# Stick-breaking heads: the value products placed behind nine products of the next projection, the weight tiles split by bank 1, 0, 2

## The chip, the cores and the metric

The kernel runs on one core of one Trainium2 chip. The metric is the device time of one execution in microseconds (us), taken as the median of several runs. Beside the times there is one execution recorded by the hardware profiler; its rows are what the profile shows. The engines are named as the profile names them: PE is TensorE (matrix products), PEld its weight loads, which run beside the products, DVE is VectorE, ACT is ScalarE, POOL is GpSimd, and SP is the engine whose queue issues most of the DMAs.

## The reference, cut to what matters

The kernel computes one transformer block on 512 tokens of width 1024. A conditioning vector gives six shift, scale and gate vectors. The normed and modulated input goes through one wide projection `w_in`, which feeds 16 stick-breaking attention heads (head size 64), 4 retention heads and two branch gates. Both branches are projected, gated, added and projected again, and a gated feed-forward with its own norm and a last norm follow. The change lies in the stick-breaking heads:

```python
def stick_breaking_attention(q, k, v):
    ...
    for i in range(s_len // BLOCK):
        end = (i + 1) * BLOCK
        ...
        z = jnp.einsum('bhtd,bhsd->bhts', qb, kb).astype(jnp.float32) * scale
        ...
        mask = s_pos[None, :] < t_pos[:, None]
        log_1m_beta = jnp.where(mask, jax.nn.log_sigmoid(-z), 0.0)
        after = lax.cumsum(log_1m_beta, axis=3, reverse=True) - log_1m_beta
        log_a = jax.nn.log_sigmoid(z) + after
        a = jnp.where(mask, jnp.exp(log_a), 0.0)
        outs.append(jnp.einsum('bhts,bhsd->bhtd', a.astype(v.dtype), vb))
    return jnp.concatenate(outs, axis=2)
```

For each head there are scores `z`, weights `a` (a product of sigmoids, taken from the right), and the sum of the values under these weights. Nothing of this arithmetic is changed.

## The kernel before, in words

Everything is float32. A product with nearly full precision is made of three products of rounded halves: a tensor is split into a high half (ACT copies it with rounding) and a low half (DVE subtracts the high half from the original), by `split` (L204 to L212, rows L206 on ACT and L208 on DVE). `mm3` (L230) multiplies high by high, high by low and low by high. `gemm` (L235) runs over the eight 128-row slices k of a weight tile and calls `mm3` for each, so 24 products of 512 columns make one projection of 128 output rows. All products pass through `mm`, whose line L228 therefore stands on nearly all PE rows; the tile names tell them apart: `ps<-h,whi` and `ps<-h,wlo` are products of a projection, `z<-q,q` scores, `ps<-con,s` and `av<-con,s` (L647) transposes, `av<-s,v` the value products.

The stick-breaking stage runs in the profile from about 480 to 670 us. `heads(h)` (L1125) is called for h = 0 to 16. One call does, for the head before it (n = h - 1), the transposes and splits (`sb_turn`, L640), then for head h the scores and sigmoids (`sb_front`, L617) and the scan (`sb_scan`, L634), and then the value products of head n (`sb_out`, L656). Between two calls stands projection work: `mix(1)` or `mix(2)` (one or two gate projections of 24 products, by `gate`, L810) or `sb_qk` (two projections, 48 products, the queries and keys of a later pair of heads). It has no connection with the head around it and gives PE something to do while DVE and ACT work on the head.

In a head, ten transposes bring the weights, a triangle of 128x128 blocks, into three PSUM tiles, called banks in the code: bank 0 (512 columns, `ps`), bank 1 (512 columns, `ps`) and bank 2 (256 columns, `av`). The blocks for key block j lie in bank 0 (j = 0), bank 1 (j = 1 and, from column 384, j = 3) and bank 2 (j = 2). Each bank is split into halves in SBUF (tag `s`), in the order 0, 1, 2 before. Eight value products follow: for each j two, one per half, of 512 - 128 j columns. They accumulate into one PSUM tile `o`, taken by `psa()`. The pool behind `psa()` has one buffer (`av=1`), and bank 2 of the transposes is taken by `psa()` too: `o` and bank 2 are the same PSUM memory, one after the other.

ACT then copies `o` out (L667), SP exchanges 64 rows (L669), and the next call of `heads` adds them up on DVE (`sb_sums`, L677).

A scheduler sets the order of the instructions on each engine when the program is built. It follows the order in which the code is written as far as its estimates of readiness allow, and fills gaps with work written later. Before, `sb_out` is written ahead of the projection; the scheduler draws 5, 6, 9 or 12 products of the projection ahead of the value products (5 for heads 0 and 1; 9 for 2, 4, 6, 8 and 10; 6 for 3, 5, 7, 9 and 11 to 14; 12 for 15).

Of the kernel before, what the change touches and what calls it, by code (L numbers as in the profile page):

```python
# [19 lines left out]
P = 128  # L20
D = 1024
S = 512
# [93 lines left out]
def kernel(  # L116
# [19 lines left out]
    def nm(s):  # L136
        uid[0] += 1
        return f"{s}_{uid[0]}"

    def ps():  # L140
        return pspool.tile([P, S], F32, tag="ps", bufs=BUFS["ps"], name=nm("ps"))

    def psa():
        return pspool.tile([P, S], F32, tag="av", bufs=BUFS["av"], name=nm("av"))
# [4 lines left out]
    def pair(tag):  # L149
        return apool.tile([P, 2, S], F32R, tag=tag, bufs=BUFS[tag], name=nm(tag))  # L150

    def tmp():
        return apool.tile([P, S], F32, tag="t", bufs=BUFS["t"], name=nm("t"))

    def otile():
        return apool.tile([P, S], F32, tag="o", bufs=BUFS["o"], name=nm("o"))
# [47 lines left out]
    def split(dst_hi, dst_lo, src, scale=1.0, eng=None):  # L204

        nc.scalar.activation(dst_hi, src, AF.Copy, scale=scale)  # L206
        if isinstance(scale, float) and scale == 1.0:
            return (eng or nc.vector).tensor_sub(dst_lo, src, f(dst_hi))  # L208
        return nc.vector.scalar_tensor_tensor(
            dst_lo, src, scale, f(dst_hi), op0=ALU.mult, op1=ALU.subtract  # L210
        )

    last_low = [None]

    def weight(key, eng=None):
        idx = WIDX[key]
        _, _, _, nk, cols = PLAN[idx]
        nc_cols = sum(n for _, n in cols)
        n = nk * nc_cols
        raw = load_raw(wp[idx], n)  # L220
        hi = wpool.tile([P, WCOLS], F32R, tag="whi", bufs=BUFS["whi"], name=nm("whi"))
        lo = wpool.tile([P, WCOLS], F32R, tag="wlo", bufs=BUFS["wlo"], name=nm("wlo"))
        last_low[0] = split(hi[:, :n], lo[:, :n], raw[:, :n], eng=eng)
        v = lambda t: t[:, :n].rearrange("p (k c) -> p k c", k=nk)
        return v(hi), v(lo)

    def mm(o, lhs, rhs, start, stop):
        return nc.tensor.matmul(o, lhs, rhs, start=start, stop=stop, skip_group_check=True).ins  # L228

    def mm3(o, lh, ll, rh, rl, start, stop):  # L230
        mm(o, lh, rh, start, False)
        mm(o, lh, rl, False, False)
        mm(o, ll, rh, False, stop)

    def gemm(o, w, acts, start=True, stop=True, t0=0, t1=S, ks=None):  # L235

        hi, lo = w
        n = len(acts)
        for k in ks or range(n):
            a = acts[k]  # L240
            ah, al = a if isinstance(a, tuple) else (a[:, 0, :], a[:, 1, :])
            mm3(o, hi[:, k, :], lo[:, k, :], ah[:, t0:t1], al[:, t0:t1],
                start and k == 0, stop and k == n - 1)


    def ada_raw(n, tag):
# [197 lines left out]
    with tc.manual_schedule(engines={nc.vector.engine, nc.scalar.engine, nc.tensor.engine}):  # L444
# [11 lines left out]
        c = sm[:, SM_C : SM_C + KT]  # L456
# [133 lines left out]
    def sb_qk(p):  # L590
        qp, kp = ps(), ps()
        gemm(qp, weight(("sq", p)), hs)
        gemm(kp, weight(("sk", p)), hs)
        low = last_low[0]
        sb_qk_store(p, qp, kp)
        return low
# [20 lines left out]
    def sb_front(h):  # L617
        q, k = sbq[h], sbk[h]
        z = [psz(), psz(), psz()]
        for i, bank, c, _ in reversed(SEG):  # L620
            w = (i + 1) * P
            for n in range(2):
                head_pe[h] = mm(z[bank][:, c : c + w], q[:, n, i * P : (i + 1) * P], k[:, 0:w],
                                n == 0 and c == 0, n == 1)
        n4, n1, b4, b1 = stick_sets[h % 2]
        for segs in ((3,), (2, 0), (1,)):
            for (t4, t1), scale in (((n4, n1), -1.0), ((b4, b1), 1.0)):
                for i, bank, c, at in (SEG[i] for i in segs):
                    w = (i + 1) * P - 1
                    t = t1 if i == 1 else t4  # L630
                    nc.scalar.activation(t[:, at : at + w], z[bank][:, c : c + w], AF.Sigmoid, scale=scale)  # L631
        return n4, n1, b4, b1

    def sb_scan(n4, n1, b4, b1):  # L634
        for n, b, d in ((n4, b4, diag), (n1, b1, diag[:, 640:896])):
            w = n.shape[-1]
            nc.vector.tensor_tensor_scan(n[:, ::-1], n[:, ::-1], d[:, ::-1], 0.0, op0=ALU.mult, op1=ALU.max)  # L637
            nc.vector.tensor_mul(b[:, 0 : w - 1], b[:, 0 : w - 1], n[:, 1:w])

    def sb_turn(n4, n1, b4, b1):  # L640
        at = [ps(), ps(), psa()]
        for i, _, _, a in reversed(SEG):
            t = b1 if i == 1 else b4
            for j in range(i + 1):
                bank, c = TGEO[j]
                c += (i - j) * P
                nc.tensor.transpose(at[bank][:, c : c + P], t[:, a + j * P : a + (j + 1) * P], ident)  # L647
        avs = []
        for bank in range(3):
            w = TBANKW[bank]  # L650
            hl = pair("s")
            ins = split(hl[:, 0, :w], hl[:, 1, :w], at[bank][:, :w])
            avs.append(hl)
        return avs, ins

    def sb_out(h, avs):  # L656
        vt = sbv[h // 4]
        o = psa()
        r, hf = (h % 4) // 2, h % 2
        for j in (3, 2, 1, 0):  # L660
            bank, c = TGEO[j]
            w = S - j * P
            v = vt[j // 2][:, j % 2, r * 256 + hf * P : r * 256 + hf * P + P]
            for i in range(2):
                mm(o[:, j * P : S], v, avs[bank][:, i, c : c + w], j == 3 and i == 0, j == 0 and i == 1)
        u, u2 = tmp(), tmp()
        nc.scalar.activation(u, o, AF.Copy)  # L667
        own, oth = (slice(0, HD), slice(HD, P)) if hf == 0 else (slice(HD, P), slice(0, HD))
        nc.sync.dma_start(u2[own], u[oth])  # L669
        late_sums.append((o_sb[h // 2], own, u, u2))  # L670
# [3 lines left out]
    def sb_sums():  # L674
        while late_sums:
            dst, own, u, u2 = late_sums.pop()
            nc.vector.tensor_add(dst[own], u[own], u2[own])  # L677
# [148 lines left out]
    def ret_mixed():  # L826
        while late_mixes:
            d, g, r = late_mixes.pop()
            nc.vector.tensor_mul(g, g, r)
            nc.sync.dma_start(spill[d], g)  # L830
# [272 lines left out]
    def sb_v(g):  # L1103

        sbv[g] = [pair("v") for _ in PI]
        for n, vt in enumerate(sbv[g]):
            nc.sync.dma_start(f(vt), vspill[2 * (g - 2) + n])
# [17 lines left out]
    def heads(h):  # L1125
        with tc.issue_after(act_table.ins):
            ins = act_table
            if h:
                if h % 8 == 1 and h > 8:
                    sb_v(2)  # L1130
                    sb_v(3)
                avs, ins = sb_turn(*fronts.pop(h - 1))
            if h < 16:
                fronts[h] = sb_front(h)
                sb_scan(*fronts[h])
            with tc.issue_after(ins.ins):
                sb_sums()
                ret_mixed()
            if h:
                if h % 2:  # L1140
                    o_sb[h // 2] = otile()
                sb_out(h - 1, avs)

    for h in range(17):
        heads(h)
        p = h // 2 + 2
        if p > 7:
            mix((1, 2, 2, 1, 2)[h - 12])
            if h == 16:
                sb_sums()  # L1150
        elif h % 2:
            mix(1)
        else:
            low_ = sb_qk(p)
            if h in (2,):
                ada_after(low_)
    ln_exp_tables()
    acts = []
    for j in range(8):
        hl = pair("q" if j < 4 else "s")  # L1160
# [3 lines left out]
    for d in range(8):  # L1164
        o = ps()
# [6 lines left out]
        hl = pair("h")  # L1172
# [326 lines left out]
    for d in range(4):  # L1499
        o = ps()  # L1500
# [191 lines left out]
    for d in FULL:  # L1692
        o = ps()
# [160 lines left out]
```

## Time and profile before

| | us |
|---|---|
| time, median of 3 runs | 1117.16 (1116.42 to 1117.90) |
| the profiled execution's own time | 1117.19 |
| its span, first to last instruction | 1115.3 |
| PE busy | 1102.8 |
| DVE busy | 871.5 |
| ACT busy | 560.7 |
| SP's DMA queue (q1), share of 16 DMA engines | 45.7% |

1.89 us of the profiled execution's own time lie outside its span. A busy PE in the table is no proof of a full PE: the end of a product is modelled and lies after the start of the next one, so that a short gap between starts does not show as idle time. Gaps are read from the starts of successive rows, and from the idle time ahead of a weight load. A timeline row has the start, the length, the engine, the line, the operation, the tiles written and read, and how many equal instructions were merged; idle time of the engine ahead of it stands in brackets.

### The profile page before, as it was taken

Reading aid. Unit: us, or ns where it says so; the run is one execution under the profiler, and the core shown is the slowest. Engines: PE = TensorE matmul, PEld = TensorE weight load, DVE = VectorE, ACT = ScalarE, POOL = GpSimd, SP = SyncE. Lnnn points to the kernel's source line nnn. Section 1 sums busy time; section 2 is a strip of 40 time slices with the busy share of each in tenths; the row PEclk is TensorE's granted clock in tenths of the full one; section 3 lists DMA queues with packets and bytes.
Section 4 is the critical chain, followed back from the end, with each engine's and each line's share of the span. In section 5 each row is a group of like instructions: output and inputs, shape, how many; then the busy total and the mean of one; then the engine's idle time right before and its main releaser. Section 6 shows DMA issues by size and latency. Waiting matters only on the chain.

```text
span 1115.3 us, 15035 instructions
## 1 busy us (share of the span) xinstructions
PE 1102.8 (99%) x5609; PEld 936.7 (84%) x5609; DVE 871.5 (78%) x1298; ACT 560.7 (50%) x925; POOL 40.6 (4%) x69
## 2 busy tenths in 40 slices
PE   9999999999999999999999999999999999999996
PEld 7888888888888888888888888889988888888886
DVE  7898966847867768488677775667999988988866
ACT  5455345445444645355565653357745544554443
POOL 0000000010020020000000000000000000000000
PEclk9999999999999999999999999999999999999999
DMA  9725751582485295888676449662444544434112
GB/s 364 297 78 185 241 188 66 169 207 77 155 179 176 78 208 187 215 237 236 177 201 166 137 152 309 240 177 58 127 138 117 149 132 132 133 113 132 58 38 76
DMA packets 59976, 181.41 MB, mean 163 GB/s; under 512 B 7424, under 2 KB 9472, under 8 KB 59904
## 3 DMA queue, kind: packets, MB, share of 16 engines
q1 hardware_dynamic: 53888, 166.30, 45.7%
q0 software_dynamic: 5472, 13.63, 7.8%
q8 instruction: 44, 0.72, 0.3%
q10 hardware_dynamic: 544, 0.52, 0.1%
q14 instruction: 28, 0.23, 0.1%
HBM read 148.97 MB, written 16.78 MB: 149 GB/s over the span
## 4 chain that ended last, share of the span: by engine, by line
PE 94%; DVE 3%; ACT 1%; DMA 0%; issue 0%; SPq 0%; DVEq 0%; ACTq 0%
PE ps L228 70%; PE z L228 14%; PE av L228 8%; PE ps L647 1%; DMA x<-xT 0%; PE z L782 0%; ACT q L1231 0%; PE av L647 0%; DVE o L1726 0%; DVE h L1541 0%; DVE t L778 0%; DVE s L1276 0%; DVE h L1276 0%; ACT h L1542 0%; DVE fin L1740 0%
## 5 line engine op out<-in xcount | busy, mean ns | idle before, releaser
L228 PE MATMUL ps<-h,whi 128*128 128x512 f32 (+1 forms) x1026 | 293.2, 372 | 0.0
L228 PEld LDWEIGHTS ps<-h,whi 128*128 128x128 f32 x1026 | 185.2, 189 | 32.2 <-issue 0.5
L206 ACT ACTIVATE whi<-raw 128x1024 fp32r<-128x1024 f32 (+1 forms) x104 | 108.7, 1046 | 196.0 <-PE ps L228 144.2
L228 PE MATMUL ps<-h,wlo 128*128 128x512 f32 (+1 forms) x513 | 187.9, 370 | 0.0
L208 DVE TENSOR_TENSOR wlo<-raw,whi 128x1024 fp32r<-128x1024 f32 (+1 forms) x104 | 124.9, 1201 | 66.8 <-ACT whi L206 66.5
L228 PEld LDWEIGHTS ps<-h,wlo 128*128 128x128 f32 x513 | 96.7, 188 | 16.6
L228 PE MATMUL ps<-s,whi 128*128 128x512 f32 x320 | 98.9, 390 | 0.0
L228 PE MATMUL ps<-q,whi 128*128 128x512 f32 (+1 forms) x368 | 98.5, 385 | 0.0
L878 DVE TENSOR_TENSOR wlo<-s,whi 128x1024 fp32r<-128x1024 f32 x46 | 56.2, 1223 | 43.2 <-ACT whi L874 43.2
L228 PEld LDWEIGHTS ps<-q,whi 128*128 128x128 f32 x368 | 68.0, 188 | 13.3
L874 ACT ACTIVATE whi<-s 128x1024 fp32r<-128x1024 f32 x47 | 49.8, 1059 | 50.2 <-PE ps L228 40.2
L228 PE MATMUL ps<-whi,h 128*128 128x512 f32 x222 | 71.8, 391 | 0.0
L228 PEld LDWEIGHTS ps<-s,whi 128*128 128x128 f32 x320 | 60.1, 188 | 12.7 <-DVE s L208 0.3
L228 PE MATMUL ps<-s,wlo 128*128 128x512 f32 x160 | 62.2, 389 | 0.0
L228 PE MATMUL ps<-q,wlo 128*128 128x256 f32 (+1 forms) x328 | 59.3, 293 | 0.0
L228 PEld LDWEIGHTS ps<-q,wlo 128*128 128x128 f32 x328 | 48.2, 190 | 3.3
L228 PEld LDWEIGHTS ps<-whi,h 128*128 128x128 f32 x222 | 41.7, 188 | 9.6 <-ACT t L1023 1.1
L228 PE MATMUL ps<-wlo,h 128*128 128x512 f32 x111 | 43.2, 389 | 0.0
L228 PE MATMUL ps<-whi,q 128*128 128x512 f32 x128 | 40.7, 389 | 0.0
L637 DVE TENSOR_TENSOR_SCAN s<-s,table 128x1024 f32<-128x1024 f32 x16 | 36.6, 2288 | 4.6 <-ACT s L631 4.5
L228 PE MATMUL z<-q,q 128*128 128x256 f32 (+3 forms) x224 | 40.1, 325 | 0.0
L228 PEld LDWEIGHTS z<-q,q 128*128 128x128 f32 x224 | 34.8, 189 | 3.0 <-DVE q L208 0.2
(353 smaller groups left out, 2187.5 us busy)
## 6 DMA issues: line engine op xcount, KB each, us to landing
raw<-wp SPq DMA_DIRECT2D x136, 512.0 KB, 3.8
araw<-wp SPq DMA_DIRECT2D x30, 512.0 KB, 4.2
s<-wp SPq DMA_DIRECT2D x24, 512.0 KB, 6.0
araw<-wada SPq DMA_DIRECT2D x18, 512.0 KB, 4.5
sraw<-wada SPq DMA_DIRECT2D x16, 512.0 KB, 9.0
q<-qp SPq DMA_DIRECT2D x32, 256.0 KB, 3.7
s<-wada SPq DMA_DIRECT2D x14, 512.0 KB, 7.2
spill<-o POOLq DMA_DIRECT2D x24, 256.0 KB, 4.4
```

What stands on the lines that cost most here:

```text
L206: nc.scalar.activation(dst_hi, src, AF.Copy, scale=scale)
L208: return (eng or nc.vector).tensor_sub(dst_lo, src, f(dst_hi))
L228: return nc.tensor.matmul(o, lhs, rhs, start=start, stop=stop, skip_group_check=True).ins
L637: nc.vector.tensor_tensor_scan(n[:, ::-1], n[:, ::-1], d[:, ::-1], 0.0, op0=ALU.mult, op1=ALU.max)
L647: nc.tensor.transpose(at[bank][:, c : c + P], t[:, a + j * P : a + (j + 1) * P], ident)
L874: nc.scalar.activation(hi, t, AF.Copy)
L878: last_low[0] = nc.vector.tensor_sub(lo, t, f(hi))
```

## The change

Two things are changed. First, `heads` no longer calls `sb_out` itself. It puts the call into a list, `due`, and `gemm` takes it from there and makes it after its third slice, that is behind nine products of the projection that comes next. Second, `sb_turn` splits the banks in the order 1, 0, 2, and `sb_out` makes the value products in the order j = 3, 1, 0, 2, so that both that read bank 1 come first, then the one of bank 0 and then the one of bank 2.

```diff
     last_low = [None]
+    due = []
...
             mm3(o, hi[:, k, :], lo[:, k, :], ah[:, t0:t1], al[:, t0:t1],
                 start and k == 0, stop and k == n - 1)
+            if k == 2 and due:
+                due.pop()()
...
-        avs = []
-        for bank in range(3):
+        avs = {}
+        for bank in (1,0,2):
             w = TBANKW[bank]
-            hl = pair("s")
+            avs[bank] = hl = pair("s")
             ins = split(hl[:, 0, :w], hl[:, 1, :w], at[bank][:, :w])
-            avs.append(hl)
         return avs, ins
...
-        for j in (3, 2, 1, 0):
+        for j in (3, 1, 0, 2):
             bank, c = TGEO[j]
             w = S - j * P
             v = vt[j // 2][:, j % 2, r * 256 + hf * P : r * 256 + hf * P + P]
             for i in range(2):
-                mm(o[:, j * P : S], v, avs[bank][:, i, c : c + w], j == 3 and i == 0, j == 0 and i == 1)
+                mm(o[:, j * P : S], v, avs[bank][:, i, c : c + w], j == 3 and i == 0, j == 2 and i == 1)
...
-                sb_out(h - 1, avs)
+                due.append(lambda: sb_out(h - 1, avs))
```

What the built programs have in a row is shown at three places. The first is PE after the scores of head 4, where the value products of head 3 come; `ps` is the projection, `h_205`, `h_245` and `h_291` are its first three slices, `s_4467`, `s_4470` and `s_4473` are the three split pairs of the head in the order in which they were made, and `v` the values. Before:

```order
L228 MATMUL ps_4515<-h_205,whi_4519 128x512 x2
L228 MATMUL ps_4515<-h_205,wlo_4520 128x512
L228 MATMUL ps_4515<-h_245,whi_4519 128x512 x2
L228 MATMUL ps_4515<-h_245,wlo_4520 128x512
L228 MATMUL av_4502<-s_4470,v_3645 128x128 x2
L228 MATMUL av_4502<-s_4473,v_3645 128x256 x2
L228 MATMUL av_4502<-s_4470,v_3511 128x384 x2
L228 MATMUL av_4502<-s_4467,v_3511 128x512 x2
L228 MATMUL ps_4515<-h_291,whi_4519 128x512 x2
L228 MATMUL ps_4515<-h_291,wlo_4520 128x512
```

The same place in the changed program:

```order
L229 MATMUL ps_4502<-h_205,whi_4506 128x512 x2
L229 MATMUL ps_4502<-h_205,wlo_4507 128x512
L229 MATMUL ps_4502<-h_245,whi_4506 128x512 x2
L229 MATMUL ps_4502<-h_245,wlo_4507 128x512
L229 MATMUL ps_4502<-h_291,whi_4506 128x512 x2
L229 MATMUL ps_4502<-h_291,wlo_4507 128x512
L229 MATMUL av_4519<-s_4467,v_3645 128x128 x2
L229 MATMUL av_4519<-s_4467,v_3511 128x384 x2
L229 MATMUL av_4519<-s_4470,v_3511 128x512 x2
L229 MATMUL av_4519<-s_4473,v_3645 128x256 x2
```

Three products of the projection have moved from behind the value products to ahead of them, and the 256-column pair, which reads the last split pair, has moved to the end. So it is for heads 3, 5, 7, 9 and 11 to 14; for heads 0 and 1 four products have moved.

The second place is PE at the value products of head 4, where nine products of the projection (`ps_4654` before, `ps_4641` now) stood ahead already. Before:

```order
L228 MATMUL ps_4654<-h_291,whi_4657 128x512 x2
L228 MATMUL ps_4654<-h_291,wlo_4658 128x512
L228 MATMUL av_4641<-s_4610,v_3650 128x128 x2
L228 MATMUL av_4641<-s_4613,v_3650 128x256 x2
L228 MATMUL av_4641<-s_4610,v_3516 128x384 x2
L228 MATMUL av_4641<-s_4607,v_3516 128x512 x2
```

The changed program at the same place:

```order
L229 MATMUL ps_4641<-h_291,whi_4644 128x512 x2
L229 MATMUL ps_4641<-h_291,wlo_4645 128x512
L229 MATMUL av_4657<-s_4607,v_3650 128x128 x2
L229 MATMUL av_4657<-s_4607,v_3516 128x384 x2
L229 MATMUL av_4657<-s_4610,v_3516 128x512 x2
L229 MATMUL av_4657<-s_4613,v_3650 128x256 x2
```

Only the order among the value products differs here; so it is for heads 2, 4, 6, 8 and 10, and for head 15 with its 12 products ahead.

The third place is DVE at the last three low halves of head 4, where `ps_4594` is bank 0, `ps_4595` bank 1 and `av_4596` bank 2. Before:

```order
L208 TENSOR_TENSOR s_4607<-ps_4594,s_4607 128x512
L208 TENSOR_TENSOR s_4610<-ps_4595,s_4610 128x512
L208 TENSOR_TENSOR s_4613<-av_4596,s_4613 128x256
```

In the changed program:

```order
L208 TENSOR_TENSOR s_4607<-ps_4595,s_4607 128x512
L208 TENSOR_TENSOR s_4610<-ps_4594,s_4610 128x512
L208 TENSOR_TENSOR s_4613<-av_4596,s_4613 128x256
```

Banks 0 and 1 have changed places; bank 2 is last as before. Apart from this, DVE, ACT and POOL have the same operations in the same order. In SP's queue one write of a gated tile (L830) now stands ahead of a load of values (L1107) instead of behind it, at two places. As for the semaphores: ahead of the first value product stood an instruction of PE that only waits (for DVE), and the product itself waited for an earlier count of PE; now the product waits for DVE itself, for the same subtraction of bank 2, and the 16 extra instructions are gone. ACT has 25 more instructions that only wait, most of them ahead of the splits, for counts of the head before.

## The prediction

> **What bounds the kernel now.** I read the page's first part, then the stretches of the heads and behind them, then PE's own waits, and last single rows.
>
> ```profile
> PE 1102.8 (99%) x5609; PEld 936.7 (84%) x5609; DVE 871.5 (78%) x1298; ACT 560.7 (50%) x925; POOL 40.6 (4%) x69
> 480.00:670.00 190.00, 189.60 (x975) 158.36 (x974) 145.97 (x178) 109.96 (x239) 0.00 (x0) 1.00 0.64 184
> PEld av L228 <- issue: 6.4, 16, 0.6
> ```
>
> PE is busy for 99% of the span and, in the stretch of the heads (columns: PE, PEld, DVE, ACT, POOL, granted clock, DMA share, GB/s), for 189.60 of 190 us at the full clock, with DVE at 146 us and ACT at 110. So PE's own sequence sets the time, and only what stretches that sequence can be won. In this stretch one wait of the weight loads is listed: the first load of the value products, 16 times, once a head, 6.4 us together. The view calls it "issue", that is, it names no releaser. The rows do. Head 3:
>
> ```profile
> 519.50 1.28 DVE L208 TENSOR_TENSOR s<-ps,s 128x512 fp32r<-128x512 f32 x2
> 520.61 0.19 PEld L228 LDWEIGHTS ps<-h,wlo 128*128 128x128 f32 x1
> 520.70 0.41 DVE L208 TENSOR_TENSOR s<-av,s 128x256 fp32r<-128x256 f32 x1
> 520.84 0.40 PE L228 MATMUL ps<-h,wlo 128*128 128x512 f32 x1
> 521.23 1.11 PEld L228 LDWEIGHTS av<-s,v 128*128 128x128 f32 x8 [0.43 <-issue]
> 522.61 0.61 PE L228 MATMUL ps<-h,whi 128*128 128x512 f32 x2
> ```
>
> The load at 521.23 follows the end of DVE's subtraction of bank 2 (520.70 + 0.41 = 521.11) by 0.12 us. The first product does not read bank 2: it reads bank 1, whose halves were done at 519.50 + 1.28 = 520.78. What it waits for is the memory of bank 2, which its output `o` takes over. Head 4, with nine products ahead already:
>
> ```profile
> 536.14 0.41 DVE L208 TENSOR_TENSOR s<-av,s 128x256 fp32r<-128x256 f32 x1
> 536.37 0.40 PE L228 MATMUL ps<-h,wlo 128*128 128x512 f32 x1
> 536.67 1.11 PEld L228 LDWEIGHTS av<-s,v 128*128 128x128 f32 x8 [0.33 <-issue]
> 538.04 0.40 PE L228 MATMUL ps<-h,whi 128*128 128x512 f32 x1
> ```
>
> The same 0.12 us: 536.55 to 536.67. Here the splits come later, because a projection's splits stand ahead of them on DVE.
>
> **What a wait costs.** A load runs ahead of its product, under the product before it, so part of the 0.43 us costs nothing. What counts is the time from the start of the last product ahead to that of the first one behind: 522.61 - 520.84 = 1.77 us for head 3, 538.04 - 536.37 = 1.67 for head 4. Without a wait the retention scores show it:
>
> ```profile
> 161.34 0.39 PE L228 MATMUL ps<-whi,qp 128*128 128x512 f32 x1
> 161.56 3.98 PE L228 MATMUL z<-q,q 128*128 128x128 f32 x24
> 165.38 0.39 PE L228 MATMUL ps<-whi,h 128*128 128x512 f32 x1
> ```
>
> These are six products each of 128, 256, 384 and 512 columns, in this order, behind a product of 512; the value products are two of each, in the same order. A third of 165.38 - 161.56 is 1.27, with the 0.22 ahead 1.50 us (estimated, rounded up). So head 3 loses 0.27 us and head 4 0.17: the listed wait less 0.16.
>
> ```profile
> 487.45 1.11 PEld L228 LDWEIGHTS av<-s,v 128*128 128x128 f32 x8 [0.38 <-issue]
> 496.83 0.76 PEld L228 LDWEIGHTS av<-s,v 128*128 128x128 f32 x6 [0.38 <-issue]
> 657.34 1.11 PEld L228 LDWEIGHTS av<-s,v 128*128 128x128 f32 x8 [0.43 <-issue]
> 618.18 1.10 PEld L228 LDWEIGHTS av<-s,v 128*128 128x128 f32 x8 [0.64 <-issue]
> 512.49 1.11 PEld L228 LDWEIGHTS av<-s,v 128*128 128x128 f32 x8 [0.33 <-issue]
> 666.77 1.11 PEld L228 LDWEIGHTS av<-s,v 128*128 128x128 f32 x8 [0.33 <-issue]
> ```
>
> Heads 0 and 1 wait 0.38 us, seven heads 0.43 (head 3 the first, 14 the last), head 11 0.64, and six 0.33 (2 the first, 15 the last).
>
> **The change, part by part.**
>
> *First term, products moved ahead.* Ten heads (0, 1, 3, 5, 7, 9, 11 to 14) get three or four more products of 0.23 us ahead, at least 0.68 us. In head 3 the load would then come at 520.84 + 0.68 = 521.52, 0.3 us after the 521.23 at which it may start today; in head 11 it would come at some 618.2, just at its 618.18. The waits vanish: 2 x 0.22 + 7 x 0.27 + 0.48 = 2.81 us. The six other heads have the same number ahead as before and keep their wait, 6 x 0.17 = 1.02 us, of which the new split order takes nothing: bank 2 is last as before. What is late next: ACT's copy of `o` and SP's exchange come 0.2 to 0.7 us later against PE. Behind that copy ACT has the next weight split:
>
> ```profile
> ACT whi L206 <- PE ps L228: 68.2, 21, 3.9
> v<-vspill SPq DMA_DIRECT2D x4, 512.0 KB, 4.5
> ```
>
> It waits for PE anyway, 68.2 us in 21 waits. If that cover were gone, some 0.5 us would be paid once per head. The swap in SP's queue, twice, delays a load of values that are used five heads later, some 60 us on; cost nothing. Used at once, they would hold PE for the 4.5 us of their landing (second row).
>
> *Second term, one instruction less.* The wait for DVE stood in an instruction of its own; now the load carries it. The row of a load that waits itself:
>
> ```profile
> 99.52 0.74 DVE L778 SCALAR_TENSOR_TENSOR t<-av,sm,t 128x512 f32<-128x512 f32 x1
> 100.32 0.31 PEld L782 LDWEIGHTS z<-con,t 128*128 128x128 f32 x3 [0.35 <-DVE t L778]
> ```
>
> 100.26 to 100.32, 0.06 us instead of 0.12. In the six heads that still wait this is worth 6 x 0.06 = 0.36 us; bounds 0 and 0.36.
>
> *Third term, the order among the value products.* Each row names the first of the products merged in it; the starts count.
>
> ```profile
> 521.51 0.63 PE L228 MATMUL av<-s,v 128*128 128x256 f32 x3
> 521.68 0.63 PE L228 MATMUL av<-s,v 128*128 128x256 f32 x3
> 521.80 0.74 PE L228 MATMUL av<-s,v 128*128 128x384 f32 x3
> 521.97 0.80 PE L228 MATMUL av<-s,v 128*128 128x384 f32 x3
> 519.63 0.68 PE L228 MATMUL ps<-h,whi 128*128 128x512 f32 x2
> 520.15 0.40 PE L228 MATMUL ps<-h,wlo 128*128 128x512 f32 x1
> 520.38 0.62 PE L228 MATMUL ps<-h,whi 128*128 128x512 f32 x2
> ```
>
> The first 256-column product behind the short ones takes 0.17 us, the second 0.12, and one of 384 0.17: loads have fallen behind in the 128-column pair, and the next product pays 0.05 us unless it is 0.17 long itself. Now a 384 follows the pair, so 0.05 us a head go: 16 x 0.05 = 0.80. The other bound: short products at the end may burden the 512 behind them. Behind scores that end at 128 columns two take 520.15 - 519.63 = 0.52 us, undisturbed 520.84 - 520.38 = 0.46. If 256 did the same, 16 x 0.06 = 0.96 would be lost and nothing won. I take +0.80, since within the 256-column pair the load keeps up (0.12 us). The Trainium skill ("TensorE: Matmul & The Clock Gate", sections "LDWEIGHTS (loading the stationary operand)" and "Back-to-back issue gap") gives a load P/1.2 ns, 107 ns for 128 columns, and an isolated warm gap of N/2.4 + 2.5 ns. By these two, taking the longer for each product, the eight last an estimated 1.19 us in any order, so this term would be nil and the time 1114.0. The 0.17 beside 0.12 us of two equal products disagrees; the order does matter in this trace.
>
> **Sum.** 2.81 + 0.36 + 0.80 = 3.97 us. The profiled execution's own time is 1117.19 (span 1115.3, 1.89 us around it), 0.03 above the median 1117.16. 1117.2 - 4.0 = **1113.2 us**, 0.36% less.
>
> **The rivals.**
>
> A. *The order gives nothing or costs.* By the bounds of the third term the gain is 3.2 (1114.0) down to 2.2 us (1115.0). For it: the reversed row above. Against: the pair rows.
>
> B. *The time is given back at the next wait.* PE reaches the next head's transposes sooner and might wait for the scan, or later for weights.
>
> ```profile
> 660.77 1.20 DVE L638 TENSOR_TENSOR s<-s,s 128x1023 f32<-128x1023 f32 x1
> 662.61 0.37 PEld L647 LDWEIGHTS ps<-con,s 128*128 128x128 f32 x2
> L206 ACTq EVENT_SEMAPHORE  x46: 17/38/38, 481.0 to 668.4; - x46
> PEld z L228 <- ACT t L1705: 0.7, 1, 0.7
> PEld z L228 <- ACT s L206: 0.5, 1, 0.5
> ```
>
> The tightest turn has 662.61 - 661.97 = 0.64 us to spare against 0.27 + 0.05 won ahead of it, and both chains start from the same transposes. From 670 us on PE's loads wait 1.2 us in all (last two rows), none for a weight. If a weight stream that isn't paced by PE took back half to all of it, the time would be 1115.2 to 1117.2.
>
> C. *All 16 waits vanish.* The first product needs bank 1 alone, which is now split first. If that set the wait, all of it would go: 6.4 - 16 x 0.16 = 3.84, plus 0.80, 1112.5 us. Against it: in head 3 bank 1 was done 0.45 us ahead of the load, and the load waited for bank 2.
>
> D. *Slower: the splits come later.* ACT has 25 more waiting instructions, most ahead of the splits, each 0.02 to 0.04 us long (third row above). If they held the splits up for real, the low halves queued behind them on DVE, and with these all 16 value products, would come later. It becomes slower than before by 0.2% if the last split comes some 0.6 us later in each head: (4.0 + 2.2) / 16 = 0.39, and 0.2 of spare time in most. Then 1119.4. At 25 x 0.04 = 1 us in all, on an engine that idles 80 of 190 us, this is far away.
>
> **How the numbers follow.** 0.2% is 2.2 us, about what a measurement of this kernel can tell from no change: under 1114.9 is faster. The forecast, 1112.4 to 1114.0 with the spread of the runs, has 0.60; A 0.17, nearly all of it still faster; B 0.13, nearly all within 0.2%; C 0.06; D 0.04. Faster 0.81, same 0.15, slower 0.04. The range 1112.2 to 1115.4 holds forecast, A and C and leaves out most of B and D.
>
> **What would show it.** In the changed profile: ten of the 16 idle times ahead of the first value product gone, six left at about 0.27 us, now with DVE as their releaser; 1.45 us from the last product ahead to the first behind where there is no wait; the first product behind the 128-column pair no longer followed by a lag; transposes still without a wait. A wait at L647, or at a projection's first load behind 670 us, would make the prediction wrong, as would any product slower than before at an unchanged place.

## The result and the profile after

The changed kernel takes 1113.83 us (median of 7 runs, 1113.17 to 1114.21), the kernel before 1116.89 us beside it (7 runs, 1116.42 to 1117.90). The ratio is 0.9973 with a 95% interval of 0.9963 to 0.9983: 3.06 us or 0.27% faster, between 1.9 and 4.1 us by the interval. 1113.2 us were forecast; the gain is 0.9 us short of the 3.97 of the sum.

The profiled execution took 1113.75 us, with a span of 1111.9. The first part of its page, and PE's waits in the stretch of the heads (us in total, times, longest):

```profile
PE 1100.0 (99%) x5609; PEld 936.9 (84%) x5609; DVE 871.8 (78%) x1298; ACT 560.9 (50%) x925; POOL 40.4 (4%) x69
PEld av L229 <- DVE s L208: 1.6, 6, 0.3
```

PE's busy time fell by 2.8 us with the same number of products, so most of a wait ahead of a product had been counted as busy. Of 16 waits ahead of the value products six are left, and the releaser now has a name, because the load itself waits. Where the time went is read from the first transpose of the heads to the first product of the projection behind them; the first two rows are of the kernel before, the last two of the changed one (start, duration, engine, line, operation):

```profile
483.79 0.38 PE L647 MATMUL ps<-con,s 128*128 128x128 f32 x2
676.31 0.62 PE L228 MATMUL ps<-q,whi 128*128 128x512 f32 x2
```

```profile
483.11 0.38 PE L650 MATMUL ps<-con,s 128*128 128x128 f32 x2
672.57 0.62 PE L229 MATMUL ps<-q,whi 128*128 128x512 f32 x2
```

192.52 us became 189.46: 3.06 us. I call this length **the heads' stage**, or the stage, below. The spans differ by 3.4 us: the stage began 0.68 us earlier, and the part behind it, up to the end, became 0.3 us longer. The stage is a better ruler than the total, since its start came between 482.9 and 485.2 us in the profiles of this study, a spread that the edits, which all lie in the stage, do not account for (one kernel, that with the own bank below, began at 485.17 in one profile and at 483.26 in another).

Within the stage I measure each head as the prediction did, from the start of the last product ahead of the value products to that of the first one behind. Summed over the 16 heads this was 27.86 us before and is 24.75 now, 3.11 less. The ten heads whose products moved went from 17.83 to 15.08, and the six others from 10.03 to 9.68. One of each kind, head 3 (moved) and head 4 (not moved), with DVE's last split, the last product ahead, the loads, and the first product behind:

```profile
519.56 0.42 DVE L208 TENSOR_TENSOR s<-av,s 128x256 fp32r<-128x256 f32 x1
520.39 0.39 PE L229 MATMUL ps<-h,wlo 128*128 128x512 f32 x1
520.40 1.46 PEld L229 LDWEIGHTS av<-s,v 128*128 128x128 f32 x8
521.90 0.63 PE L229 MATMUL ps<-h,whi 128*128 128x512 f32 x2
...
534.75 0.42 DVE L208 TENSOR_TENSOR s<-av,s 128x256 fp32r<-128x256 f32 x1
535.00 0.40 PE L229 MATMUL ps<-h,wlo 128*128 128x512 f32 x1
535.22 1.33 PEld L229 LDWEIGHTS av<-s,v 128*128 128x128 f32 x8 [0.27 <-DVE s L208]
536.61 0.62 PE L229 MATMUL ps<-h,whi 128*128 128x512 f32 x2
```

In head 3 the split is done at 519.98 and the load starts at 520.40, straight behind the load ahead of it: no wait, and 521.90 - 520.39 = 1.51 us. In head 4 the split ends at 535.17, the load starts at 535.22, and the eight products take 536.61 - 535.00 = 1.61 us.

What was open after this: whether the third term of the sum, the order among the value products, gave anything; whether the move alone does the rest; whether the memory of bank 2 is what the six heads still wait for; and what happens when products are moved further.

### The profile page after: what moved, and what is told of

Same layout as the page of the kernel before. It is cut to its first block, busy times and chain, and to the rows that moved or that the text cites. A ratio compares the mean times of both kernels' runs of the same rounds, so it can differ in the third digit from the quotient of the medians.

```text
span 1111.9 us, 15043 instructions
## 1 busy us (share of the span) xinstructions
PE 1100.0 (99%) x5609; PEld 936.9 (84%) x5609; DVE 871.8 (78%) x1298; ACT 560.9 (50%) x925; POOL 40.4 (4%) x69
## 4 chain that ended last, share of the span: by engine, by line
PE 91%; DVE 5%; ACT 2%; DMA 1%; issue 1%; SPq 0%; DVEq 0%; ACTq 0%
PE ps L229 68%; PE z L229 14%; PE av L229 8%; PE ps L650 1%; DMA araw<-wada 0%; DMA x<-xT 0%; DVE araw L262 0%; PE z L784 0%; PE av L650 0%; DVE wlo L208 0%; ACT q L1233 0%; DVE o L1728 0%; DVE h L1543 0%; DVE s L208 0%; DVE sraw L396 0%
```

## The experiments

The first four were measured beside each other and beside the kernel before, then three, then two. Every diff is against the changed kernel.

### 1. The move alone

```diff
-        for bank in (1,0,2):
+        for bank in range(3):
...
-        for j in (3, 1, 0, 2):
+        for j in (3, 2, 1, 0):
...
-                mm(..., j == 3 and i == 0, j == 2 and i == 1)
+                mm(..., j == 3 and i == 0, j == 0 and i == 1)
```

> The value products are put behind nine products of the next projection as in the change, but the banks are split in the old order 0, 1, 2 and the value products stand in the old order 128, 256, 384, 512 columns. Its waiting instruction ahead of the value products is there again. Theory (the gain is the waits, the order among the value products is worth nothing): where there is no wait, 1.50 to 1.51 us from the last product ahead to the first behind, as in the changed kernel; the six heads that still wait go back from 1.61 to 1.67 us; time about 0.3 us above the changed kernel, 1114.1 us beside 1116.9. Rival (the order does save 0.05 us a head, and something else cost as much in the changed kernel): 1.55 us in the heads without a wait, time about 1114.9 us.

1114.52 us (median of 11 runs), ratio 0.9982 (0.9972 to 0.9991). PE's wait in the heads, and head 4:

```profile
PEld av L229 <- issue: 2.0, 6, 0.3
...
535.66 0.41 DVE L208 TENSOR_TENSOR s<-av,s 128x256 fp32r<-128x256 f32 x1
535.90 0.40 PE L229 MATMUL ps<-h,wlo 128*128 128x512 f32 x1
536.19 1.11 PEld L229 LDWEIGHTS av<-s,v 128*128 128x128 f32 x8 [0.34 <-issue]
537.58 0.63 PE L229 MATMUL ps<-h,whi 128*128 128x512 f32 x2
```

Six waits are left, as after the whole change, but they are as long as before: the split ends at 536.07 and the load starts 0.12 us later, and no releaser is named. The six heads take 10.04 us (10.03 before). The ten moved heads take 15.04 us, against 15.08 with the new order: without a wait, **the old order is as fast as the new one**. The heads' stage is 189.91 us, 2.61 less than before; the heads' sum says 27.86 - 25.08 = 2.78. So the move gives nearly all of the gain, and the new order adds 10.04 - 9.68 = 0.36 us in the six heads that wait, and by this ruler nothing in the ten. A longer ruler, from the last product ahead in head 11 to that in head 14, shows a trace of it: 654.22 - 615.86 = 38.36 us in the changed kernel and 655.44 - 617.06 = 38.38 here, under 0.01 us a head.

### 2. The order alone

```diff
-                due.append(lambda: sb_out(h - 1, avs))
+                sb_out(h - 1, avs)
```

> The banks are split in the order 1, 0, 2 and the value products stand in the new order, but they are called where they were before, with no products moved behind. Theory (the first value product waits for the memory of bank 2, which is split last in either order): all 16 waits stay; only the waiting instruction is gone, 0.06 us a head, so about 1.0 us less than before, 1115.9 us beside 1116.9, with idle times of 0.27 us and more ahead of all 16 first loads. Rival (bank 1 split first lets the first product start): no idle time is left at the first load, and the time falls by 3 to 4 us, to 1113 or 1114.

1116.70 us (11 runs), ratio 0.9997 (0.9988 to 1.0005): the total doesn't resolve it. The waits, and head 3:

```profile
PEld av L229 <- DVE s L208: 5.7, 16, 0.6
...
519.75 1.28 DVE L208 TENSOR_TENSOR s<-ps,s 128x512 fp32r<-128x512 f32 x2
520.95 0.41 DVE L208 TENSOR_TENSOR s<-av,s 128x256 fp32r<-128x256 f32 x1
521.09 0.40 PE L229 MATMUL ps<-h,wlo 128*128 128x512 f32 x1
521.41 1.34 PEld L229 LDWEIGHTS av<-s,v 128*128 128x128 f32 x8 [0.37 <-DVE s L208]
522.80 0.63 PE L229 MATMUL ps<-h,whi 128*128 128x512 f32 x2
```

All 16 waits are there. The two banks that the first six products read are split by 519.75 + 1.28 = 521.03, and still the load starts only at 521.41, 0.05 us behind the split of bank 2 (521.36). Splitting bank 1 first does nothing for a product whose output stands in bank 2. The load starts 0.05 us behind the split instead of 0.12 in all 16 heads, and 13 heads take 0.05 to 0.06 us less than before (1.71 instead of 1.77 us here). Heads 0, 1 and 11 take 0.06, 0.04 and 0.01 us more: in the first two the scheduler put four products ahead instead of five, and in head 11 the split ended 0.07 us later against the product ahead. So the heads' sum is 27.23, 0.63 less than before, and the stage 191.87, 0.65 less, where 1.0 was expected. The split order and the product order were not separated by a run, so which of the two lets the load carry the wait is left open here.

### 3. An output with a bank of its own

```diff
-        o = psa()
+        o = ps()
```

> The changed kernel, with the output of the value products in a buffer of the four that projections and banks 0 and 1 share, instead of in the one buffer that bank 2 uses. Theory (it is the shared memory that sets the wait of the six heads): their idle time of 0.27 us is gone, 1.51 us instead of 1.61 in all 16 heads, about 0.6 us less than the changed kernel, 1113.2 us beside 1116.9. Rival (the wait is for the data, the last split): the 0.27 us stay at the first load or move to the load that reads bank 2. A second rival: four buffers are too few, and PE waits for one at a projection's or a transpose's first product, which would cost more than it gives.

1113.09 us (5 runs), ratio 0.9966 (0.9953 to 0.9978). No wait of a load is listed any more in the stretch of the heads; all 16 heads take 1.508 us, 24.13 together, and the stage 188.79 us. So it is the shared memory of bank 2 that the six heads waited for, not the data. Against the changed kernel the heads' sum is 0.62 us shorter, which the totals don't tell apart; the stage does (189.46 - 188.79 = 0.67). It was measured once more below.

### 4. Behind twelve products

```diff
-            if k == 2 and due:
+            if k == 3 and due:
```

> The changed kernel with the value products behind twelve products of the projection instead of nine. Theory: three products of 0.23 us cover the 0.27 us that six heads still wait; all 16 idle times are gone, 1.51 us in each head, about 0.6 us less than the changed kernel, 1113.2 us beside 1116.9. Rival (the won time is given back because ACT's copy, the exchange and the next head come later): a wait appears at the transposes or further on, and the time is the changed kernel's or more, 1113.8 us or above.

1113.71 us (5 runs), ratio 0.9968 (0.9956 to 0.9981). The waits, and the load of head 2:

```profile
PEld av L229 <- DVE s L208: 0.5, 2, 0.3
...
512.88 1.33 PEld L229 LDWEIGHTS av<-s,v 128*128 128x128 f32 x8 [0.21 <-DVE s L208]
```

Two waits are left where none was expected, in head 2 (listed 0.21 us, takes 1.552) and in head 15, which had twelve products ahead from the start (1.605). In head 2 the splits themselves came late: ahead of them DVE had waited 1.65 us for a DMA (`araw<-wada`, L262), against 0.74 in the changed kernel. The 14 others take 1.504, so this figure belongs to the new order as well as to the old one. The sum is 24.21, the stage 188.94 us: three more products of 0.23 us ahead are about as good as the extra bank.

### 5. The longest products first

```diff
-        o = psa()
+        o = ps()
...
-        for j in (3, 1, 0, 2):
+        for j in (0, 1, 2, 3):
...
-                mm(..., j == 3 and i == 0, j == 2 and i == 1)
+                mm(..., j == 0 and i == 0, j == 3 and i == 1)
```

> As the kernel with the value products' output in a buffer of its own (no wait left), with the value products in the order 512, 384, 256, 128 columns. Theory (each product takes as long as the longer of its own columns and one weight load of 0.11 us, in any order, so what a short product leaves over is paid by the product behind it, whatever its length): 1.50 to 1.51 us from the last product ahead to the first two behind it less their own time, that is, the 0.06 us that the pair of 128 columns owes shows at the projection's first product, and from the last product ahead to the second product behind it is 1.74 us as before. Rival (a short product's lag can be hidden behind a long one): 0.05 us more in each head, since a product of 512 follows the pair of 128 here in the projection and could have hidden it as well, or less if it does.

1113.50 us, one run, so nothing can be said from the total. One wait is listed in the heads, 0.17 us in head 15. Head 4, where no wait disturbs it: the last product ahead, the value products, and what follows them.

```profile
535.39 0.39 PE L229 MATMUL ps<-h,wlo 128*128 128x512 f32 x1
535.62 1.37 PE L229 MATMUL ps<-s,v 128*128 128x512 f32 x8
536.84 0.67 PE L229 MATMUL ps<-h,whi 128*128 128x512 f32 x2
537.35 0.39 PE L229 MATMUL ps<-h,wlo 128*128 128x512 f32 x1
```

By the ruler used so far this order looks 0.07 us faster: 536.84 - 535.39 = 1.45. But the two products behind take 537.35 - 536.84 = 0.51 us, where two of 512 columns elsewhere take 0.46. To the third product behind it is 1.96 us. The same place of the kernel with its own bank and the order of the change (from its second profile, below):

```profile
535.02 0.39 PE L229 MATMUL ps<-h,wlo 128*128 128x512 f32 x1
535.25 1.44 PE L229 MATMUL ps<-s,v 128*128 128x128 f32 x8
536.53 0.62 PE L229 MATMUL ps<-h,whi 128*128 128x512 f32 x2
536.99 0.39 PE L229 MATMUL ps<-h,wlo 128*128 128x512 f32 x1
```

536.99 - 535.02 = 1.97 us. To the second product behind, the theory had 1.74 us as before; 1.72 were measured, and 1.74 with the order of the change. That difference goes too: from the last product ahead in head 11 to that in head 14 it is 654.26 - 615.88 = 38.38 us here and 653.82 - 615.46 = 38.36 with the order of the change, and the stage is 188.92 us against 188.79 there. The order shifts 0.05 us from one product to another and gives nothing.

### 6. Behind all 24 products

```diff
-            if k == 2 and due:
+            if k == 7 and due:
```

> The changed kernel with the value products behind all 24 products of the projection. In eight heads (0, 2, 4, 6, 8, 10, 11, 14) the next head's transposes then stand directly behind them. Theory (too late is as bad as too early, because the transposes of bank 2 take the memory of the output, which ACT must have copied out): no wait ahead of the value products, but some 0.7 us at the transposes in these eight heads, 5 to 6 us in all, time 1118 to 1119 us beside 1116.6. Rival (no wait comes in their place): 1113 us.

1115.88 us (10 runs), ratio 0.9991 (0.9981 to 1.0). The waits:

```profile
PEld av L650 <- ACT t L669: 2.0, 7, 0.3
PEld ps L650 <- ACT g L818: 0.7, 1, 0.7
```

Now the transposes wait. In seven turns it is a transpose into bank 2 that waits, the memory that ACT still has to copy `o` out of (L669). The eighth wait, ahead of the transposes of head 3, is another one:

```profile
507.94 1.23 DVE L262 SCALAR_TENSOR_TENSOR araw<-araw,cact 128x1024 f32<-128x1024 f32 x1 [2.86 <-DMA araw<-wada]
515.37 1.20 DVE L641 TENSOR_TENSOR s<-s,s 128x1023 f32<-128x1023 f32 x1
516.68 0.53 PEld L650 LDWEIGHTS ps<-con,s 128*128 128x128 f32 x5 [0.69 <-ACT g L818]
516.71 0.74 PE L650 MATMUL ps<-con,s 128*128 128x128 f32 x5 [0.52 <-DVE s L641]
```

The load's row names ACT, but its idle time ends 0.11 us behind DVE's long multiplication of the scan (515.37 + 1.20 = 516.57), and PE's own row names that step: the weights of the head were late, and ahead of their scan DVE had waited 2.86 us for the same DMA as in the fourth experiment. Whether the placing of the value products made that DMA late was not tried. The stage is 191.16 us, 1.70 longer than after the change, so over half of the gain is given back; some 0.67 us of what was lost stand in that one wait (head 2 takes 2.18 us, the others 1.51). The places were as expected, the cause in seven of the eight, and the price a third: 0.3 us for each of the seven waits at bank 2, instead of 0.7. In the built program the transposes into bank 2 stand seventh and eighth of the ten in these turns, so ACT's copy has more time.

### 7. Its own bank, without the move

```diff
-        o = psa()
+        o = ps()
...
-                due.append(lambda: sb_out(h - 1, avs))
+                sb_out(h - 1, avs)
```

> The kernel with the value products' output in a buffer shared with the projections, splits by bank 1, 0, 2, but the value products are called ahead of the projection as before the change. The scheduler then puts them directly behind the scores, with no product ahead. Theory (products ahead are what covers the splits; a separate memory and the split order alone do not): every head waits for the splits, 0.6 us or more in ten heads and above 1 us in the six in which the splits come later, together some 15 us, time about 1125 to 1130 us. Rival (bank 1 first, in a memory of its own, is enough): no more than 0.2 us a head, time 1113 to 1116 us.

1121.59 us (5 runs), ratio 1.0038 (1.0024 to 1.0052): slower than before. The waits:

```profile
PEld ps L229 <- DVE s L208: 4.0, 9, 0.5
PEld ps L229 <- DVE qp L208: 2.4, 5, 0.5
PEld ps L229 <- ACT s L206: 1.1, 1, 1.1
```

With nothing that holds the value products at a place, the scheduler puts them directly behind the scores, where the splits are not ready, and the waits for DVE return. The stage is 197.15 us, 8.4 more than with the same bank and the move. The direction was as expected, the size not (15 us and 1125 to 1130 were): the listed waits are 0.48 us in 13 of the heads, where 0.6 and above 1 us had been put. In heads 2, 4, 6, 8 and 10 three products of the projection stand between the first value product and the others; there no value product waits, but the first of these three does, here in head 4:

```profile
535.10 0.68 DVE L208 TENSOR_TENSOR qp<-ps,qp 128x512 fp32r<-128x512 f32 x1
535.83 0.30 PEld L229 LDWEIGHTS ps<-h,whi 128*128 128x128 f32 x2 [0.48 <-DVE qp L208]
```

Its load starts 0.05 us behind the end of DVE's split of an earlier projection, whose result it does not read. What it can need from that split is one of the four `ps` buffers, of which `o` now holds one; this reading was not tested by itself. So two costs are mixed in this run. Without the move the shared bank had done some good: it kept the value products back (1116.70 us with it, second experiment).

### 8 and 9. The changed kernel and the own bank again

> The changed kernel once more, beside the next one on the same chip. Expected: 1113.8 us beside 1116.7, six idle times of 0.27 us ahead of the value products, 189.5 us from the first transpose to the first product of the projection behind the heads.

> The changed kernel with the value products' output in a buffer of the four that the projections use, once more. Expected, if what the stage shows holds for the time: 0.6 to 0.7 us below the changed kernel, about 1113.1 us, 188.8 us from the first transpose to the first product of the projection behind the heads. Rival: the two cannot be told apart, or the shared buffers cost as much elsewhere.

The changed kernel took 1114.12 us (9 runs, ratio 0.9974, 0.9964 to 0.9984), the one with its own bank 1112.89 (5 runs, ratio 0.9965, 0.9952 to 0.9978). The stage of the changed kernel was 189.44 us; that of the own bank, from its rows:

```profile
483.26 0.38 PE L650 MATMUL ps<-con,s 128*128 128x128 f32 x2
672.05 0.62 PE L229 MATMUL ps<-q,whi 128*128 128x512 f32 x2
```

188.79, as in the first profile, 0.65 us less. Head 4 of the own bank shows why (DVE's last split, the loads):

```profile
534.78 0.41 DVE L208 TENSOR_TENSOR s<-av,s 128x256 fp32r<-128x256 f32 x1
535.02 1.45 PEld L229 LDWEIGHTS ps<-s,v 128*128 128x128 f32 x8
```

The load starts at 535.02, straight behind the one ahead and 0.17 us before the split of bank 2 has ended (535.19). Twice the ratio to the kernel before is lower than that of the changed kernel (0.9966 against 0.9973, and 0.9965 against 0.9974 measured side by side); the intervals overlap, so the totals alone don't prove it, but the stage does, with the same length in both profiles. It is the shortest stage of the versions run, 0.13 us below the fifth experiment and 0.15 below the fourth; the totals of these three are not told apart.

## Why the prediction was right, and where not

**What bounds the kernel: right.** PE's sequence sets the time; the 3.06 us by which its stage of heads became shorter are the size of the difference of the medians, 3.06. That both agree to the last digit is luck: the interval of the ratio is 2 us wide, and the spans of the two profiles differ by 3.4.

**First term, products moved ahead: right.** 2.81 us forecast. By the heads' sum the move alone gave 2.78 and by the stage 2.61 (first experiment). The waits vanished in just the ten heads named, and stayed in the six, which lost 1.67 - 1.50 = 0.17 us each, as worked out.

**Second term, one instruction less: right in size and place.** 0.36 forecast, 10.04 - 9.68 = 0.36 measured between the first experiment and the whole change. The lag from the end of DVE's split to the load fell from 0.12 to 0.05 us. The second experiment shows that this part comes with the order and not with the move.

**Third term, the order among the value products: wrong.** The step that failed is "so 0.05 us a head go: 16 x 0.05 = 0.80". Measured: 1.508 us a head in the new order and 1.504 in the old one where there is no wait, that is 0.00 and not 0.05, and under 0.01 by the longer ruler of the first experiment. The 1.45 us named as the sign of it never appeared in that order. The reading behind it was of two rows, 0.17 us for the first product of 256 columns behind the short pair and 0.12 for the second. The lag of the pair is real, but I took it that a product of 384 columns, being 0.17 us long, would hide it. It doesn't. Rows of narrow windows in head 3 of the changed kernel; each names the first of the products merged in it, and its start counts:

```profile
520.63 0.56 PE L229 MATMUL av<-s,v 128*128 128x128 f32 x3
520.80 0.56 PE L229 MATMUL av<-s,v 128*128 128x384 f32 x2
521.02 0.56 PE L229 MATMUL av<-s,v 128*128 128x384 f32 x2
```

Here the first 384 takes 521.02 - 520.80 = 0.22 us, where an undisturbed one takes 0.17: it pays the same 0.05 us that the 256 paid in the old order. In the fifth experiment a product of 512 columns pays it. The rows look as if the starts behind short products were recorded 0.05 us early, whichever product follows; the trace can't tell that from a real delay, but the sum over the group is the same. With the term left out the sum is 3.17 us and the time 1114.0; 1113.83 and 1114.12 were measured.

The Trainium skill ("TensorE: Matmul & The Clock Gate", sections "LDWEIGHTS (loading the stationary operand)" and "Back-to-back issue gap") had made this term nil, and I set it aside for those two rows. On the order the runs agree with it (1.504 and 1.508 us). The 1.19 us that I estimated from its figures for the eight products are short, though: in the new order 521.90 - 520.63 = 1.27 us were measured.

**The rivals.** A, that the order gives nothing or costs, is what happened, at its end of nothing, which I had put at 1114.0; the other end, a loss of 0.96, fell. B, that the time is given back at the next wait, fell for all but a small part. No transpose waits after the change; at the tightest turn the load now starts 0.35 us behind the scan's long multiplication, where 0.64 us was the least before. Behind the heads PE's loads have the two waits that they had, and one that is new:

```profile
PEld z L229 <- ACT t L1707: 0.7, 1, 0.7
PEld z L229 <- ACT s L206: 0.5, 1, 0.5
PEld ps L229 <- DVE t L1371: 0.4, 1, 0.4
```

The new one is a load of a projection at 824.88 us, for a sum on DVE. A wait at such a place was named as a sign that the prediction is wrong; it is there, but small: the part behind the stage is 0.3 us longer in this profile, nearly all of it at this wait. In a second profile of the changed kernel (the eighth experiment) it is listed with 0.2 us and that part is 0.1 longer, in the kernel with the own bank it is not listed, and with the move alone it has 0.5 us. Why PE comes to be ahead of DVE there was not tried. The mechanism of B exists, but elsewhere: the sixth experiment finds it at 24 products ahead, at the transposes, seven times for ACT's copy and once for the scan. C, that all 16 waits vanish since bank 1 is split first, fell in the second experiment, where all 16 stayed. What makes them vanish is the bank of `o` (third experiment). D, that ACT's added waiting instructions hold up the splits, fell: the 25 stand in the order-only kernel as well (332 in all, 307 before and with the move alone), whose heads' sum is 0.63 us below that of before, not above it. The covers that the first term relied on held: from the heads on, no wait of PE for a weight or for a load of values has appeared. Ahead of the heads one has: at 123.29 us, far from the edits, PE waits 0.50 us for a weight's low half, which it did not in the profile before. A product slower than before at an unchanged place was named as a sign against the prediction too; the part ahead of the stage is 0.68 us shorter all the same, and the cause of this wait was not looked for.

**The chances.** The time lies in the range, 0.6 us above the forecast, just where the case without the third term was put. By its mechanism this is the upper end of rival A, which had 0.17, with the first two terms of the case that had 0.60. That the number falls within that case's 1112.4 to 1114.0 is partly luck: the interval was wide enough to hold the sum with and without its wrong term.

## What to carry to other kernels

Before reordering the readers of some data, look at what the waiting instruction writes: here the first product waited for the memory of its output, not for its input, and only more work ahead of it (0.27 us a head) or another bank (0.65 us more in all) removed that. Compare groups of products as a whole, from an undisturbed start to a start two or three products behind; the interval of a single product next to short ones misleads. And work is moved only as far as the next user of the same memory allows: nine products ahead won 3.1 us, twelve 3.6, 24 only 1.4 (by the stage, each with the new order).

## What the runs showed of the hardware

- The order of products of different lengths gave nothing: eight value products with no wait ahead take 1.50 to 1.51 us, counted with the product ahead, whether the two short ones are followed by 256 or 384 columns. With the short ones last, 1.45, and 0.05 more in the products behind them. From head 11 to head 14 the three orders take 38.36 to 38.38 us.
- A load that carries its wait itself starts 0.05 us after the end of DVE's split; with the wait in an instruction of its own ahead of it, 0.12 us, and then the view of waits names no releaser.
- The listed idle time of a load is more than what is lost: 0.27 us listed in head 4 after the change, 1.61 - 1.51 = 0.10 lost.
